# Keys and values of eight sampled tokens: float32 products in four column groups and a summing product

## The chip, the core and the metric

The kernel runs on one core of a Trainium2 chip. The metric is the device time of one launch in microseconds (us). Three runs of the kernel before gave 896.83, 897.12 and 897.53 us; the median is 897.12 us.

## What is computed

One layer of a hybrid decoder for 512 new prompt tokens and 8 sampled tokens (one new token for each of 8 sequences with a cache of 1,024 tokens). The part that the change touches is the projection of keys and values, cut from the reference:

```python
h = modulate(x, lp['norm_attn'], sh1, sc1)           # (512 + 8 tokens) x 1024
proj = jnp.dot(h, lp['w_in'])                         # 1024 x 1816
sizes = [D_SSM, D_ATTN, D_KV, D_KV, D_KV, D_KV, D_KV, D_KV]
u, q, k_c, v_c, k_s, v_s, k_w, v_w, g = jnp.split(proj, offsets, axis=-1)
```

`k_c, v_c` feed the compressed branch of the attention, `k_s, v_s` the selected one, `k_w, v_w` the window; each pair is 256 columns wide. `g` are 24 gate columns. Everything is float32 in the reference. The projected keys and values are outputs too.

## The kernel before

All tensors of the layer lie with 128 features in partitions and tokens in columns. `hH` and `hL` hold the normed input as a high and a low part in a rounded float32 form (`F32R`): 8 blocks of 128 features (`KT`), 520 columns each, the last 8 of them the sampled tokens (`T:NT`). `split` makes such a pair: ScalarE rounds a copy, VectorE subtracts. A product of two such pairs is three matmuls (high by high, high by low, low by high). Plain float32 operands are also taken by TensorE; the trace then shows two records for one matmul.

`kv_proj(c)` is called for c = 0, 1, 2 (compressed, selected, window). It loads 1 MB of `w_in` into a raw buffer (`wkv`, 1024 features by 256 columns; for c = 2 also the gate columns `rg`), splits it into `wH` and `wL`, and then, for five groups of tokens t, multiplies tokens (stationary) by weights (moving): t = 0 to 3 are 128 prompt tokens each, t = 4 is the 8 sampled tokens. Each t takes 24 matmuls, three for each of 8 feature blocks. For t = 4 the result is 8 rows by 256 (or 280) columns; ScalarE copies it to `kvs`, from which it goes to the outputs and later into the attention of the sampled tokens.

Raw buffers come from a pool of three (`rawt`), used in turn by blocks of `w_ada` (`wada`, for the modulation, `ada`), blocks of the cache (`rc`), `wkv` and others. A load into a raw buffer waits until the last reader of the block before it is done. The small buffer `mrow` has one copy; `ada` puts its sums there, and the query projection its `ql`. `ada(s)` multiplies the condition vectors by a block of `w_ada` in float32: the 8 feature blocks go in turn to four groups of 32 output partitions, and the four groups are added after a transpose (`padt`) by a reduction on VectorE.

A scheduler decides the order on each engine: it takes the instructions as written, with their dependences and its own estimate of durations, and fills each engine's queue. So a change in one place shifts what stands beside it, and what follows. Every queue (PE, ACT, DVE, POOL, and SP which issues most loads) is worked off in order, and a waiting instruction holds those behind it.

The stages in the order of time: set-up, first compressed cache blocks and input norm (to about 93 us in the profiled execution); projection `pj` of the state space input, and `kv_proj(0)` (to 136 us); the state space stage in eight steps `qd`, with the cache blocks of the sampled tokens, `ada` and the compressed branch beside it (to about 250 us), in whose last part `kv_proj(1)` and `kv_proj(2)` lie; the queries (to about 296 us); the attention (to about 450 us); then the output projection and the two large products of the MLP.

Of the state space stage these pieces matter: `uscr` is a scratch in DRAM, to which the input `u` is written (from `ut` for the prompt, from `uT` for the sampled tokens); ten loads `U<-uscr` bring it back in another layout; `pvs` (line 792) is the first product of a step that needs `U`; `mscr` and `Tz` are a second way through DRAM for each step.

In the attention, 16 rounds of the prompt (scores `pst`, exponentials on ACT, transposes `ptp`, values `po`) alternate with the work of the sampled tokens (`pkT`, `pS`, `ppt`, `poS`, `pov`) and the gates of the state space output (`pg`).

Of the kernel before, what the change touches and what calls it, by code (L numbers as in the profile page):

```python
# [9 lines left out]
F32 = mybir.dt.float32  # L10
# [3 lines left out]
ALU = mybir.AluOpType  # L14
AX = mybir.AxisListType

P = 128
D = 1024
T = 512
NB = 8  # L20
NT = T + NB
HB = NT // 2
KT = D // P
# [13 lines left out]
def body(tc, i, o, dbg=None):  # L37
    nc = tc.nc
# [18 lines left out]
    def pst(tag, name):  # L57
        return bank["tile"].tile([P, 512], F32, tag=tag, name=name, bufs=bank["tags"][tag])
# [13 lines left out]
    ident = cst.tile([P, P], F32, name="ident")  # L72
# [44 lines left out]
    wp = ctx.enter_context(tc.tile_pool(name="wp", bufs=1, reuse_waits="tile"))  # L117
    k2x = ExitStack()
    keep2 = k2x.enter_context(tc.tile_pool(name="keep2", bufs=1, reuse_waits="tile"))
    mod = keep.tile([P, 48, 9], F32, name="mod")  # L120
    xs = keep.tile([P, KT, NB], F32, name="xs")
# [78 lines left out]
        nc.scalar.activation(oh, hf, AF.Identity, bias=sh)  # L200
        nc.vector.scalar_tensor_tensor(ol, hf, sh, oh, ALU.add, ALU.subtract)

    def affine_samples(pool, oh, ol, x, bs, A, sh):

        th = pool.tile([P, KT, NB], F32, tag="ths", name="ths")
        nc.vector.tensor_tensor(th, x, bs.unsqueeze(1).to_broadcast([P, KT, NB]), ALU.mult)
        nc.vector.tensor_tensor(th, th, A[:, :, 1:9], ALU.mult)
        nc.vector.tensor_tensor(th, th, sh[:, :, 1:9], ALU.add)
        split(oh[:, :, T:NT], ol[:, :, T:NT], th)
# [287 lines left out]
    for lv in range(3):  # L497
        n = 1 << lv
# [73 lines left out]
    hH = hp.tile([P, KT, NT], F32R, name="hH")  # L572
    hL = hp.tile([P, KT, NT], F32R, name="hL")

    def x_tile(k):
        px = pst("tr", "px")
        for t in range(4):
            nc.tensor.transpose(px[:, t * P : (t + 1) * P], xr[t][:, k * P : (k + 1) * P], ident)
        xk = p0.tile([P, T], F32, tag="xk", name="xk", bufs=4)
        nc.scalar.copy(xk, px)  # L580
        nc.gpsimd.dma_start(xscr[:, k], xk)
        return xk

    affine_samples(p0, hH, hL, xs, bc[1], A1, mod[:, 0:8])
    for k in range(KT):
        affine_split(p0, hH[:, k, 0:T], hL[:, k, 0:T], x_tile(k), bc[0], A1[:, k, 0:1], mod[:, k, 0:1])
    p0x.close()
# [33 lines left out]

    onames = ("cmp", "slc", "win")

    def kv_proj(c):
        c0 = 1024 + 256 * c
        r = rawt("wkv").rearrange("p (k c) -> p k c", k=KT)
# [5 lines left out]
        ws = []  # L632
# [7 lines left out]
        for t in range(5):  # L640
            tok = slice(t * P, t * P + (P if t < 4 else NB))
            mp = P if t < 4 else NB
            ps = pst("pj", "pkv")
            for k in range(KT):
                wh, wl = ws[k // 4]
                for n, (x, w) in enumerate(((hH, wh), (hH, wl), (hL, wh))):
                    nc.tensor.matmul(ps[0:mp, 0:nw], x[:, k, tok], w[:, k % 4], start=(k == 0 and n == 0),  # L647
                                     stop=(k == KT - 1 and n == 2))
            if t == 4:
                nc.scalar.copy(kvs[:, c * 256 : (c + 1) * 256], ps[0:NB, 0:256])  # L650
                if c < 2:
# [944 lines left out]
```

## Time and profile before

| | |
|---|---|
| median of 3 runs | 897.12 us |
| profiled execution | 896.29 us, of it 894.6 us from the first to the last instruction (span) |
| TensorE busy (matmuls) | 844.3 us, 94% |
| VectorE busy | 525.0 us, 59% |
| ScalarE busy | 388.2 us, 43% |
| GpSimd busy | 65.2 us, 7% |
| chain that ended last | PE 86%, DMA 6%, ACT 3%, DVE 2% |
| DMA traffic | 122.36 MB, 137 GB/s on the mean |

The share of busy time says that TensorE is the engine to look at first, and the chain (the work that ended last, followed back from the end) says how much of the span TensorE's own work set. Line numbers, as L647, are those of the kernel before. A name as `pkv<-wH,hH` reads: tile `pkv` is written from `wH` and `hH`. The duration of one matmul in the trace reaches past the start of the next one, since matmuls are pipelined; what a matmul takes from TensorE is therefore read from the distance of two starts.

### The profile page before, as it was taken

What the parts mean: (1) busy time and instruction counts of PE and PEld (TensorE: products, weight loads), DVE (VectorE), ACT (ScalarE), POOL (GpSimd) and SP (SyncE); (2) the same over time, 40 slices, a digit from 0 to 9 for tenths busy, and PEclk for the clock granted to TensorE, in tenths of its full rate; (3) what the DMA queues carried; (4) which work ended last, traced back from release to release, by engine and by line L of the source; (5) the groups of instructions that cost most, each with busy time, mean ns of one, the idle gap of its engine ahead of it and who ended that gap; (6) DMA issues with size and microseconds to landing.
All of it is one profiled execution on the core that took longest, in us unless ns stands there. A gap on an engine that the chain in (4) does not pass through costs nothing.

```text
span 894.6 us, 16415 instructions
## 1 busy us (share of the span) xinstructions
PE 844.3 (94%) x6517; PEld 747.3 (84%) x6517; DVE 525.0 (59%) x1413; ACT 388.2 (43%) x880; POOL 65.2 (7%) x147
## 2 busy tenths in 40 slices
PE   3799998999999899999889999999999999999995
PEld 2567897788998676756579999999999999999995
DVE  6676656759747975667578964443233444434534
ACT  2545326634435656546655554441111344433422
POOL 6001201000134200100000000000000000000000
PEclk9999999999999999999999999999999999999998
DMA  8956678366456620303257552333333333332202
GB/s 294 318 193 217 194 169 239 123 204 194 127 179 206 203 95 1 142 1 142 78 206 227 161 189 85 95 95 95 95 95 95 95 95 95 96 88 70 79 1 95
DMA packets 111836, 122.36 MB, mean 137 GB/s; under 512 B 24500, under 2 KB 91880, under 8 KB 109584
## 3 DMA queue, kind: packets, MB, share of 16 engines
q1 hardware_dynamic: 102256, 89.71, 33.0%
q0 software_dynamic: 5488, 29.99, 9.8%
q10 hardware_dynamic: 4016, 1.62, 0.7%
q8 instruction: 51, 0.84, 0.4%
q14 instruction: 25, 0.20, 0.1%
HBM read 112.47 MB, written 13.03 MB: 140 GB/s over the span
## 4 chain that ended last, share of the span: by engine, by line
PE 86%; DMA 6%; ACT 3%; DVE 2%; issue 1%; SPq 0%; ACTq 0%; DVEq 0%
PE pdn L1401 21%; PE pup L1401 20%; PE pj L605 5%; PE pwo L1401 5%; PE pkv L647 5%; PE ph L387 5%; DMA wada<-w_ada 5%; PE pada L334 2%; PE ptp L1246 2%; PE po L1253 2%; PE pS L1032 2%; PE pg L1273 2%; PE pst L1217 2%; PE pys L819 2%; PE pkT L1023 1%; PE pst L1218 1%
## 5 line engine op out<-in xcount | busy, mean ns | idle before, releaser
L1401 PE MATMUL pdn<-hidL,wH 128*128 128x256 f32 (+1 forms) x480 | 136.1, 284 | 0.0
L1401 PE MATMUL pdn<-hidH,wL 128*128 128x256 f32 (+1 forms) x480 | 135.9, 283 | 0.0
L1401 PE MATMUL pdn<-hidH,wH 128*128 128x256 f32 (+1 forms) x480 | 135.4, 282 | 0.0
L1401 PE MATMUL pup<-h2L,wH 128*128 128x256 f32 (+1 forms) x480 | 135.0, 282 | 0.0
L1401 PE MATMUL pup<-h2H,wL 128*128 128x256 f32 (+1 forms) x480 | 135.0, 282 | 0.0
L1401 PE MATMUL pup<-h2H,wH 128*128 128x256 f32 (+1 forms) x480 | 134.1, 283 | 0.0
L1401 PEld LDWEIGHTS pup<-h2L,wH 128*128 128x128 f32 x480 | 90.4, 188 | 0.8 <-DVE rs_t L97 0.8
L1401 PEld LDWEIGHTS pdn<-hidH,wL 128*128 128x128 f32 x480 | 90.6, 189 | 0.0
L1401 PEld LDWEIGHTS pdn<-hidL,wH 128*128 128x128 f32 x480 | 90.4, 188 | 0.1
L1401 PEld LDWEIGHTS pup<-h2H,wL 128*128 128x128 f32 x480 | 90.4, 188 | 0.0
L1401 PEld LDWEIGHTS pdn<-hidH,wH 128*128 128x128 f32 x480 | 90.4, 188 | 0.0
L1401 PEld LDWEIGHTS pup<-h2H,wH 128*128 128x128 f32 x480 | 89.6, 188 | 0.0
L63 ACT CAST wH<-wdn 128x1024 fp32r<-128x1024 f32 x30 | 31.5, 1050 | 114.0 <-PE pdn L1401 104.1
L64 DVE TENSOR_TENSOR wL<-wup,wH 128x1024 fp32r<-128x1024 f32 x30 | 36.7, 1224 | 58.1 <-ACT wH L63 58.1
L64 DVE TENSOR_TENSOR wL<-wdn,wH 128x1024 fp32r<-128x1024 f32 x30 | 36.8, 1225 | 54.2 <-ACT wH L63 54.2
L387 PE MATMUL ph<-xc,w 128*128 128x256 f32 (+2 forms) x320 | 65.4, 356 | 1.2 <-DVE xc L377 0.7
L387 PEld LDWEIGHTS ph<-xc,w 128*128 128x128 f32 x320 | 52.8, 203 | 12.9 <-issue 6.4
L63 ACT CAST wH<-wup 128x1024 fp32r<-128x1024 f32 x30 | 31.5, 1050 | 48.0 <-PE pup L1401 37.6
L1479 ACT ACTIVATE rl<-pup 128x256 f32<-128x256 f32 (+1 forms) x64 | 24.4, 384 | 48.9 <-PE pup L1401 48.8
L375 ACT COPY xc<-pxc 64x256 f32<-64x256 f32 x96 | 32.1, 366 | 20.8 <-DVE xc L377 18.2
L1410 DVE SCALAR_TENSOR_TENSOR xT<-pdn,mod,xT 128x256 f32<-128x256 f32 x32 | 15.2, 479 | 43.2 <-PE pdn L1401 43.2
L1480 DVE TENSOR_TENSOR rl<-rl 128x256 f32<-128x256 f32 (+1 forms) x64 | 27.1, 425 | 22.6 <-ACT rl L1479 22.6
(557 smaller groups left out, 2023.9 us busy)
## 6 DMA issues: line engine op xcount, KB each, us to landing
wada<-w_ada SPq DMA_DIRECT2D x20, 1024.0 KB
wup<-w_up SPq DMA_DIRECT2D x16, 1024.0 KB
wdn<-w_down SPq DMA_DIRECT2D x16, 1024.0 KB
wo<-w_out SPq DMA_DIRECT2D x8, 1024.0 KB
wada<-w_ada SPq DMA_DIRECT2D x8, 512.0 KB
rwin<-state_win SPq DMA_DIRECT2D x4, 1024.0 KB
new_win_sample<-state_win POOLq DMA_DIRECT2D x2, 2044.0 KB, 8.9
wkv<-w_in SPq DMA_DIRECT2D x3, 1024.0 KB
```

Of the source, the lines that this page charges most:

```text
L63: nc.scalar.copy(h, src)
L64: nc.vector.tensor_tensor(l, src, h, ALU.subtract)
L334: nc.tensor.matmul(ps[k % 4 * 32 : k % 4 * 32 + 32], cT[:, k], rs[k // kp][:, k % kp], start=(k < 4), stop=(k >= 4))
L375: nc.scalar.copy(dst[:, :, :, hf], srcv[:, :, :, hf])
L387: nc.tensor.matmul(phv[:, lo:hi, 0:w], w1[n][:, r_], xc[n][:, lo:hi, r_ % 8, off : off + w], start=(r_ == 0), stop=(r_ == 15))
L605: nc.tensor.matmul(ps[:, 0:HB], w[:, k], x[:, k, hc], start=(k == 0 and n == 0), stop=(k == KT - 1 and n == 2))
L647: nc.tensor.matmul(ps[0:mp, 0:nw], x[:, k, tok], w[:, k % 4], start=(k == 0 and n == 0), stop=(k == KT - 1 and n == 2))
L819: nc.tensor.matmul(py[:, c], Tz[:, :, :, g].rearrange("p t c -> p (t c)"), U[:, qd * GQ + g], start=True, stop=False)
L1032: nc.tensor.matmul(S[b4 * 32 : b4 * 32 + 32], q4[:, 4 * grp + b4], kts[b4], start=True, stop=True)
L1401: nc.tensor.matmul(ps[:, 0 : b - a], w, x[:, a:b], start=first and n == 0, stop=last and n == 2)
L1479: nc.scalar.activation(rl, ps[:, 0 : b - a], AF.Relu)
L1480: nc.vector.tensor_tensor(rl, rl, rl, ALU.mult)
```

## The change

For t = 4 the 24 matmuls are replaced. A new tile `hs` holds the 8 sampled tokens in plain float32, padded with zeros to 32 columns for each of the 8 feature blocks. Eight float32 matmuls multiply `hs` (128 features by 32 tokens, stationary) by the raw block `wkv` itself (moving, 256 columns); feature block k goes to the group of 32 output partitions k mod 4, so each group adds two blocks. For c = 2 eight more of 24 columns do the gates from `rg`. ScalarE copies the 128 rows into `part`, which uses the buffer of `mrow`; then one float32 matmul with `sel` (128 by 8: which rows belong to token p) adds the four groups into a new PSUM tile `pks`. The rest of t = 4 is as before. `hs` is filled where the split of the sampled tokens is made; `sel` is a sum over `ident`.

```diff
-        th = pool.tile([P, KT, NB], F32, tag="ths", name="ths")
+        if th is None:
+            th = pool.tile([P, KT, NB], F32, tag="ths", name="ths")
...
+    hs = hp.tile([P, KT, 32], F32, name="hs")
+    nc.gpsimd.memset(hs, 0.0)
...
-    affine_samples(p0, hH, hL, xs, bc[1], A1, mod[:, 0:8])
+    affine_samples(p0, hH, hL, xs, bc[1], A1, mod[:, 0:8], hs[:, :, 0:NB])
...
+    sel = p1.tile([P, NB], F32, name="sel")
+    nc.vector.tensor_reduce(sel, ident.rearrange("p (q x) -> p x q", x=32)[:, 0:NB], AX.X, ALU.add)
...
-            for k in range(KT):
-                wh, wl = ws[k // 4]
-                for n, (x, w) in enumerate(((hH, wh), (hH, wl), (hL, wh))):
-                    nc.tensor.matmul(ps[0:mp, 0:nw], x[:, k, tok], w[:, k % 4], start=(k == 0 and n == 0),
-                                     stop=(k == KT - 1 and n == 2))
+            if t == 4:
+
+                for c0, src in ((0, r),) + (((256, rg),) if c == 2 else ()):
+                    for k in range(KT):
+                        q = slice(k % 4 * 32, k % 4 * 32 + 32)
+                        nc.tensor.matmul(ps[q, c0 : c0 + src.shape[2]], hs[:, k], src[:, k], start=(k < 4), stop=(k >= 4))
+                part = wp.tile([P, 520], F32, tag="mrow", name="part")[:, 0:nw]
+                nc.scalar.copy(part, ps[:, 0:nw])
+                ps = pst("pj", "pks")
+                nc.tensor.matmul(ps[0:NB, 0:nw], sel, part, start=True, stop=True)
+            else:
+                for k in range(KT):
+                    wh, wl = ws[k // 4]
+                    for n, (x, w) in enumerate(((hH, wh), (hH, wl), (hL, wh))):
+                        nc.tensor.matmul(ps[0:mp, 0:nw], x[:, k, tok], w[:, k % 4], start=(k == 0 and n == 0),
+                                         stop=(k == KT - 1 and n == 2))
```

The scheduler's order differs from the first of these places on until the MLP. Three places matter for the prediction.

The first is SP's queue where `u` goes out to `uscr` and comes back as `U`, at the end of `kv_proj(0)`. Before:

```order
L619 DMA uscr<-uT 128x8
L330 DMA wada<-w_ada 128x4x512
L618 DMA uscr<-ut 128x512
L724 DMA U<-uscr 16x32x8
L725 DMA U<-uscr 16x32x8
L722 DMA U<-uscr 16x32x64 x8
L772 DMA mscr<-M_1541 128x64
```

Now:

```order
L623 DMA uscr<-uT 128x8
L742 DMA U<-uscr 16x32x8
L622 DMA uscr<-ut 128x512
L743 DMA U<-uscr 16x32x8
L740 DMA U<-uscr 16x32x64 x8
L331 DMA wada<-w_ada 128x4x512
L790 DMA mscr<-M_1532 128x64
```

The 1 MB block `wada` (first half of `ada(5)`) goes into the raw buffer that held `wkv` of c = 0; it stood ahead of the last write to `uscr`, and now stands behind the ten loads of `U`.

The second place is TensorE's queue where the summing product of c = 1 and of c = 2 stands, and ScalarE's at c = 2. TensorE at c = 1 now:

```order
L656 MATMUL pkv<-wkv,hs 32x256 x5
L700 MATMUL pkt<-ident,kvt 128x128 x2
L785 MATMUL pbb<-ident,BP 128x128 x4
L660 MATMUL pks<-part,sel 8x256
L665 MATMUL pkv<-wH,hH 128x280
```

TensorE at c = 2 now (`pj` is the first product of the queries):

```order
L656 MATMUL pkv<-wkv,hs 32x256 x8
L656 MATMUL pkv<-rg,hs 32x24 x8
L700 MATMUL pkt<-ident,kvt 128x128 x2
L660 MATMUL pks<-part,sel 8x280
L609 MATMUL pj<-hH,wH 128x260
```

ScalarE at c = 2 before (from the copies of t = 3 to those of t = 4):

```order
L675 COPY kvt<-pkv 128x256
L677 COPY Vx<-pkv 128x128
L103 ACTIVATE gates<-pkv 128x24
L678 DMA new_win_prompt<-kvt 128x2x64
L679 DMA new_win_prompt<-Vx 128x128
L63 CAST wH<-wq 128x1024
L650 COPY kvs<-pkv 8x256
```

and now:

```order
L693 COPY kvt<-pkv 128x256
L695 COPY Vx<-pkv 128x128
L103 ACTIVATE gates<-pkv 128x24
L63 CAST wH<-wq 128x1024
L696 DMA new_win_prompt<-kvt 128x2x64
L697 DMA new_win_prompt<-Vx 128x128
L63 CAST KH<-pkt 128x2x128
L658 COPY part<-pkv 128x280
L668 COPY kvs<-pks 8x256
```

At c = 0 fourteen other matmuls stand between the products and their sum, at c = 1 six, at c = 2 two; and at c = 2 a cast of weights, two issues of stores and a cast of `KH` stand ahead of the copy `part` on ScalarE.

The third place is the end of the attention on TensorE. Before, from the last work of the sampled tokens (`pov`) to the output projection (`pwo`):

```order
L1127 MATMUL pov<-ident,ovS 128x128
L1253 MATMUL po<-PT,Vx 64x512 x2
L1246 MATMUL ptp<-ident,pe 128x128 x2
L1246 MATMUL ptp<-ident,pe_4992 128x128 x2
L1246 MATMUL ptp<-ident,pe 128x128
L1253 MATMUL po<-PT,Vx 64x384 x2
L1253 MATMUL po<-PT,Vx 64x128 x2
L1253 MATMUL po<-PT,Vx 64x256 x2
L1329 MATMUL po<-etc,Vbd 128x512
L1401 MATMUL pwo<-mixH,wH 128x256
```

Now a part of what stands between `pov` and `pwo`, 15 to 26 rows ahead of `pwo`:

```order
L1271 MATMUL po<-PT,Vx 64x384 x2
L1271 MATMUL po<-PT,Vx 64x128 x2
L1264 MATMUL ptp<-ident,pe 128x128
L1264 MATMUL ptp<-ident,pe_4854 128x128
L1264 MATMUL ptp<-ident,pe 128x128 x2
L1235 MATMUL pst<-KH,QS 128x256
L1236 MATMUL pst<-KL,QS 128x256
L1237 MATMUL pst<-cmaskr,identr 128x128
L1271 MATMUL po<-PT,Vx 64x256 x2
L1264 MATMUL ptp<-ident,pe 128x128 x3
```

Before, 12 rows lie from `pov` to `pwo`, the values of the last pair of heads; now 43 rows do, with the last scores of the prompt among them. The work of the sampled tokens has moved to earlier rounds.

## Rows read from the trace of the kernel before

**Rows 1.** The page's head: busy time, share of the span, instructions.
```profile
PE 844.3 (94%) x6517; PEld 747.3 (84%) x6517; DVE 525.0 (59%) x1413; ACT 388.2 (43%) x880; POOL 65.2 (7%) x147
```
**Rows 2.** Busy time by stage: each engine's us and instructions, then granted clock, DMA.
```profile
93.00:136.00 43.00, 43.00 (x364) 40.41 (x362) 25.01 (x68) 13.07 (x27) 4.25 (x8) 1.00 0.70 172
136.00:180.00 44.00, 40.29 (x262) 33.69 (x259) 30.24 (x79) 28.61 (x82) 4.87 (x14) 1.00 0.60 189
180.00:296.00 116.00, 114.60 (x851) 101.91 (x848) 82.40 (x207) 50.12 (x130) 27.10 (x65) 1.00 0.57 175
296.00:450.00 154.00, 143.96 (x1041) 94.48 (x1037) 103.36 (x323) 93.52 (x256) 9.42 (x19) 1.00 0.28 101
```
**Rows 3.** Timeline of TensorE, t = 4 of c = 0: start, us, what.
```profile
130.40 0.28 PE L647 MATMUL pkv<-wL,hH 128*8 128x256 f32 x1
...
132.72 0.28 PE L647 MATMUL pkv<-wH,hH 128*8 128x256 f32 x1
```
**Rows 4.** Timeline of TensorE, t = 4 of c = 2 and what follows.
```profile
263.33 0.29 PE L647 MATMUL pkv<-wH,hH 128*8 128x280 f32 x1
...
266.40 0.38 PE L682 MATMUL pkt<-ident,kvt 128*128 128x128 f32 x2
266.54 0.36 PE L605 MATMUL pj<-hH,wH 128*128 128x260 f32 x1
```
**Rows 5.** Timeline of TensorE: a float32 product in four column groups, and what follows.
```profile
134.96 1.07 PE L334 MATMUL pada<-wada,cT 128*32 128x512 f32 x8
135.96 0.44 PE L368 MATMUL pxc<-ident,rc 128*128 128x128 f32 x2
```
**Rows 6.** Timeline of TensorE: float32 products over all columns; 32-column products.
```profile
194.20 3.70 PE L387 MATMUL ph<-xc,w 128*128 128x256 f32 x16
197.74 0.34 PE L820 MATMUL pys<-Sx,Cb 128*128 128x80 f32 x2
...
438.44 1.08 PE L1121 MATMUL poS<-rslc,ptS 128*32 128x128 f32 x32
```
**Rows 7.** Timeline of ScalarE around t = 4 of c = 2.
```profile
263.67 0.38 ACT L675 COPY kvt<-pkv 128x256 f32<-128x256 f32 x1
264.08 0.39 ACTq L678 DMA_DIRECT2D new_win_prompt<-kvt  x1
264.09 0.22 ACT L103 ACTIVATE gates<-pkv 128x24 f32<-128x24 f32 x1
264.51 0.77 ACTq L679 DMA_DIRECT2D new_win_prompt<-Vx  x1
265.32 1.05 ACT L63 CAST wH<-wq 128x1024 fp32r<-128x1024 f32 x1 [1.01 <-PE pkv L647]
```
**Rows 8.** Timeline of SP, where `uscr` is written and `U` read.
```profile
120.61 0.38 SPq L330 DMA_DIRECT2D wada<-w_ada  x1
121.15 0.39 SPq L618 DMA_DIRECT2D uscr<-ut  x1
127.00 5.11 SPq L722 DMA_DIRECT2D U<-uscr  x8
```
**Rows 9.** Timeline of TensorE's weight loads, 137 to 142 us.
```profile
138.48 0.97 PEld L792 LDWEIGHTS pvs<-U,Bb 128*128 128x128 f32 x8 [1.67 <-issue]
141.53 0.16 PEld L334 LDWEIGHTS pada<-wada,cT 128*32 128x32 f32 x8 [1.31 <-DMA wada<-w_ada]
```
**Rows 10.** Timeline of TensorE at the end of the attention.
```profile
436.39 1.09 PE L1049 MATMUL ppt<-ident,tS 128*128 128x128 f32 x8 [1.06 <-ACT tS L1010]
441.05 0.42 PE L1123 MATMUL poS<-kvs,pnw 8*32 8x128 f32 x8
448.59 0.65 PE L1253 MATMUL po<-PT,Vx 128*64 128x256 f32 x4 [1.94 <-ACT PT L1249]
```
**Rows 11.** Busy time by stretch, end of the attention, columns as in rows 2.
```profile
443.00:450.00 7.00, 4.42 (x27) 2.08 (x23) 4.90 (x10) 5.66 (x14) 0.72 (x1) 0.98 1.06 368
450.00:453.00 3.00, 3.00 (x13) 2.48 (x13) 3.00 (x12) 2.00 (x6) 0.00 (x0) 0.50 1.04 386
```

More of the change, by code (lines that the diff above doesn't have):

```diff
@@ L201, in affine_split, with affine_samples @@
         nc.vector.scalar_tensor_tensor(ol, hf, sh, oh, ALU.add, ALU.subtract)
-    def affine_samples(pool, oh, ol, x, bs, A, sh):
-        th = pool.tile([P, KT, NB], F32, tag="ths", name="ths")
+    def affine_samples(pool, oh, ol, x, bs, A, sh, th=None):
+        if th is None:
+            th = pool.tile([P, KT, NB], F32, tag="ths", name="ths")
         nc.vector.tensor_tensor(th, x, bs.unsqueeze(1).to_broadcast([P, KT, NB]), ALU.mult)
```

## The prediction

> **What bounds the kernel now.** I read the page's head first, then busy time by stage, then the timelines of single places. The head shows TensorE busy for 844.3 of 894.6 us [rows 1]. By stage the reader should see where that is true without a gap: from 93 to 136 us TensorE is busy all the time, from 180 to 296 us for 114.60 of 116 us; from 136 to 180 us it idles for 3.7 us, in the attention (296 to 450 us) for 10.0 us [rows 2]. So a matmul taken away in `kv_proj` shortens the run by its own time, as long as the other engines keep up, and two of the three places of t = 4 lie in stretches where nothing but TensorE counts. The attention is another case: TensorE waits there, on and off, for ScalarE and VectorE, which are busy for 93.52 and 103.36 us of its 154 [rows 2], and what counts is which work stands beside which.
>
> **What goes.** 24 matmuls at each place. At c = 0 the rows 130.40 and 132.72 are 20 matmuls apart: 2.32 us / 20 = 0.116 us each, 24 of them 2.78 us [rows 3]; c = 1 has the same shape. At c = 2, with 280 columns, 24 starts lie from 263.33 to 266.40: 3.07 us [rows 4].
>
> **What comes on TensorE.** The eight products of `hs` by `wkv` are of a form that the trace has: `ada` multiplies 32 stationary columns by float32 weights in four column groups. One group of four with 512 columns (eight records) takes from 134.96 to 135.96, 1.00 us [rows 5]; eight with 256 columns move the same number of columns. I take 1.00 us. The upper bound is eight products one after the other at the full-width rate: 16 float32 records of 256 columns take from 194.20 to 197.74, 0.22 us a record, 0.44 us a matmul [rows 6], so 3.5 us; the lower is 0.5 us, the 16 records at 0.034 us, as in the 32 of `poS` in 1.08 us [rows 6]. The row of `ada` differs from the new products in the column count alone, so it decides. The summing product is one full-width float32 matmul, 0.44 us (0.48 us with 280 columns). The eight gate products of 24 columns are 16 records; at 0.034 us that is 0.5 us.
>
> So c = 0 and c = 1 go from 2.78 to 1.44 us, 1.34 us less each. c = 2 goes from 3.07 to 1.00 + 0.50 + 0.48 = 1.98 us, 1.09 us less.
>
> **The wait that is added.** `pks` waits for `part`, ScalarE's copy of the products (0.38 us, as the copy `kvt` of the same shape [rows 7]), and TensorE's queue stands behind it. At c = 0 fourteen other matmuls are between, and at c = 1 two transposes and four `pbb`, 6 x 0.11 us = 0.7 us: enough for the copy. At c = 2 only two transposes (0.14 us [rows 4]) are between, and ScalarE has more to do first. Counted from 263.33 us: the products end at 263.33 + 1.50 = 264.83, the transposes at 264.97. ScalarE ends `gates` at 264.31; the cast of 1,024 weight columns takes 1.05 us (to 265.36), the issue of the store of `Vx` behind it 0.77 us, of `kvt` 0.4 us (they began at 264.08 and held the queue to 265.28 [rows 7]; now they follow the start of the cast, to about 265.5), then `KH` and `part` with some 0.3 us each: 266.1 us. TensorE waits 1.1 us, does the sum to 266.6, and `pj` starts at 266.6 instead of 266.54 [rows 4]. So c = 2 saves nothing: I take 0, between a loss of 0.5 us (the cast waits for its buffer as well) and the full 1.09 us.
>
> If the copy decided at c = 0 and c = 1 too, products, copy and sum would stand in a row, 1.00 + 0.40 + 0.44 = 1.84 us, and each of the two would give 0.94 us instead of 1.34: 0.8 us less in the sum.
>
> The Trainium skill speaks for that case ("TensorEngine Tiling (Array Packing)", PSUM Bottleneck): packing products into column groups speeds TensorE up but not the copy out of PSUM, which may then be the limit. By that rule the sum below would be -1.7 instead of -2.5 us; the rows of ScalarE and the order bear it out at one place of three.
>
> **What moves.** `wkv` is now read until t = 4, so the raw buffer of c = 0 comes free some 10 us later, and the block of `w_ada` that goes into it moves behind the loads of `U`. Before, that 1 MB was issued at 120.61 us, just ahead of the last write to `uscr` at 121.15 us, and the loads of `U` could start at 127.00 us only, 5.85 us after it [rows 8]; TensorE then waited 1.67 us at `pvs`, the first reader of `U`, and 1.31 us for the next block of `w_ada` [rows 9]. Without 1 MB ahead the write should land some 3 us sooner and `U` with it. The block itself comes later, at about 131.3 us (end of the products) instead of 120.61; the one that TensorE waited for at 141.53 was issued 5.4 us before, so this one is there at 136.7 us, about when its product now comes up. Bounds: 2.98 us gained, if both waits go and none comes; 1.5 us lost, if TensorE meets the late block as early as it met the old one (134.96 us [rows 5]). I take 0.8 us gained, since TensorE gets there 1.3 us earlier and uses part of the head start up.
>
> `mrow` now holds `part` too, so the transposes of `ada(4)` move behind the sum of c = 0, and a reduction on VectorE follows before the next `ada` product: one exchange of about 0.4 us, inside the term above. The zeros of `hs` (GpSimd, 7% busy [rows 1]), `sel` and the wider copy are hidden beside TensorE.
>
> **The attention's new order.** Nothing is added there; the same work is dealt out in another way. Before, the last round still had 5 us of the sampled tokens' matmuls beside it (from `ppt` at 436.39 to `poS` at 441.05), and TensorE even so waited 1.06 and 1.94 us [rows 10], and the granted clock was 0.50 for the 3 us from 450 us, the 1.2 GHz level, after a stretch in which TensorE was busy for 4.42 of 7 us [rows 11]. Now two rounds have nothing beside them; what is gone from there fills earlier rounds. Of 10.0 us of idle time [rows 2] I let a quarter be at stake, 2.5 us either way, and take 1.0 us lost, since the tail is where ScalarE and VectorE have the least in hand.
>
> **Sum**, against the profiled execution: -1.34 - 1.34 + 0 - 0.8 + 1.0 = -2.5 us, 896.29 to 893.8 us. The median of the runs is 0.83 us above the profiled execution, so 894.6 us.
>
> **The rivals.**
> *The saving is lost in waits.* The sums wait for ScalarE at c = 0 and c = 1 too (0.8 us less, worked out with the wait), the head start of `U` is spent on the late block (0 instead of 0.8), and the attention takes 1.0 us. For it: PE's queue is in order and c = 2 shows how one cast is enough; against it: six and more matmuls stand between at the other two. -2.68 + 0.8 + 1.0 = -0.9 us: 896.2 us, no change that can be told.
> *The attention pays more.* The place is from the last `pov` to `pwo`. If the two bare rounds run at the pace of ScalarE and VectorE, the 5 us of matmuls that stood in the last round are no longer hidden, and another spell at the 1.2 GHz level, as the 3 us from 450 us (1.5 us lost), can follow. It decides as soon as it costs over 3.5 us; with 5 us, -1.34 - 1.34 - 0.8 + 5 = +1.5, with the clock +3.0 us: 898.6 to 900.1 us. For it: 12 rows have become 43 behind `pov`. Against it: what moved fills idle time elsewhere.
> *The state space stage starts 3 us sooner and keeps it.* Then both waits of rows 9 go: -2.68 - 2.98 + 0 = -5.7 us: 891.5 us. For it: SP's queue; against it: from 180 us on TensorE is nearly full, so a chain that is early has nothing to give.
>
> **How the numbers follow.** The forecast 0.46, lost in waits 0.23, slower attention 0.19, early stage 0.12. A measurement here tells 0.2% from no change, 1.8 us: faster is below 895.3, slower above 898.9 us. The forecast's own spread is 893 to 896.2 us; of its 0.46, 0.08 lie above 895.3. Faster: 0.38 of it, 0.12, and 0.02 of the case of the waits, 0.52; same: 0.08 and the other 0.21, 0.29; slower: 0.19. The range that leaves out 2 in 10 reaches from 891.2 to 899.8 us; the likeliest case alone holds 893 to 896.2.
>
> **What would show it.** Eight products of `hs` in about 1.0 us and sums of 0.44 us; a gap ahead of `pks` at c = 2 of about 1 us and none at c = 0 and c = 1; `U` loads issued near 124 us and `pvs` near 136 us instead of 138.48; the stage's end some 2 us sooner; the attention as long as before within 2.5 us; from `pwo` on the same length. I am wrong if the column groups don't run beside each other (products of 2 us and more), if `pada` waits for the late block, or if the attention differs by more than 3 us.

## The result and the profile after

The changed kernel is slower. Four runs gave 905.44, 908.79, 912.67 and 917.11 us, median 910.73 us; the kernel before gave a median of 896.98 us beside them (895.37 to 897.53). The ratio is 1.0158, 95% interval 1.0123 to 1.0194. The prediction was 894.6 us, with a range of 891.2 to 899.8 us: wrong in sign, and its range missed too.

The profiled execution is the one of 917.11 us; its head answers to [rows 1], with the granted clock in 40 slices below:

```profile
PE 857.3 (94%) x6515; PEld 756.5 (83%) x6515; DVE 528.6 (58%) x1414; ACT 390.5 (43%) x883; POOL 65.0 (7%) x148
...
PEclk9999999996999989999999999999999999999998
```

TensorE is busy for 13.0 us more than before, although it has less to do, and the tenth slice of the clock (206 to 229 us) stands at 6 tenths, the fifteenth at 8. Where the time went is read from stretches that begin and end at the same matmul in both kernels: the first `pkv` of c = 0, the last `pj`, the first `pwo`, the first `pup` and the first `pdn`. The windows of the kernel before (stretch, us, then busy us and instructions of PE, PEld, DVE, ACT, POOL, then granted clock, DMA share, GB/s); the third row is the last part of the second, from the last `pov` on:

```profile
118.20:295.47 177.27, 172.16 (x1259) 151.71 (x1259) 123.91 (x324) 82.68 (x219) 31.44 (x76) 1.00 0.61 177
295.47:449.81 154.34, 144.30 (x1041) 94.36 (x1041) 103.69 (x324) 93.82 (x256) 9.95 (x23) 1.00 0.28 100
442.29:449.81 7.52, 4.55 (x27) 2.09 (x27) 5.33 (x13) 6.18 (x14) 0.96 (x1) 0.99 1.04 352
449.81:503.47 53.66, 52.08 (x414) 50.78 (x413) 44.80 (x129) 28.63 (x52) 0.00 (x0) 0.97 0.61 197
503.47:602.85 99.38, 98.95 (x823) 95.18 (x822) 57.22 (x133) 45.13 (x98) 0.00 (x0) 1.00 0.40 122
```

The same stretches of the changed kernel, and four short ones that are spoken of further down:

```profile
116.08:303.93 187.85, 182.69 (x1261) 156.70 (x1261) 120.77 (x315) 82.08 (x220) 26.29 (x68) 0.94 0.56 163
303.93:465.33 161.40, 146.56 (x1042) 97.61 (x1041) 110.12 (x338) 96.28 (x260) 14.62 (x31) 0.96 0.34 116
446.09:465.33 19.24, 14.04 (x80) 7.97 (x79) 12.67 (x38) 13.78 (x35) 0.00 (x0) 0.91 0.66 232
465.33:521.33 56.00, 52.06 (x414) 51.06 (x412) 45.44 (x129) 29.83 (x55) 0.00 (x0) 0.97 0.47 151
521.33:623.66 102.33, 100.92 (x821) 96.87 (x821) 56.02 (x130) 44.85 (x97) 0.00 (x0) 0.98 0.37 114
...
131.85:134.28 2.43, 0.01 (x1) 0.04 (x1) 2.32 (x6) 1.67 (x5) 0.00 (x0) 1.00 1.05 374
134.28:141.10 6.82, 6.42 (x29) 4.36 (x29) 2.87 (x9) 3.88 (x12) 0.32 (x1) 0.50 0.26 67
209.40:212.80 3.40, 3.40 (x29) 3.08 (x26) 3.37 (x10) 1.40 (x3) 0.61 (x2) 1.00 0.72 226
212.80:229.80 17.00, 17.00 (x84) 15.41 (x86) 9.31 (x26) 3.67 (x7) 0.47 (x3) 0.50 0.34 107
```

The span grew by 915.4 - 894.6 = 20.8 us: -2.1 up to the first `pkv` (where the kernel before had 3.4 us at a granted clock of 0.50 and the changed one none), +10.6 to the last `pj`, +7.1 in the attention, +2.3 in the output projection, +2.9 (2.95) to the first `pdn`, and nothing behind it. Three things are to be seen.

First, the places that the change edits are not where the time went. TensorE's timeline of the changed kernel (start, us, engine, line, operation, tile, form, count; in brackets the idle time before it and what ended it):

```profile
128.26 1.07 PE L656 MATMUL pkv<-wkv,hs 128*32 128x256 f32 x16
129.26 0.40 PE L784 MATMUL pm<-C,BP 128*128 128x16 f32 x2
...
131.25 0.60 PE L660 MATMUL pks<-part,sel 128*8 128x256 f32 x2
...
134.27 1.95 PE L810 MATMUL pvs<-U,Bb 128*128 128x72 f32 x8 [2.42 <-DVE BP L772]
...
274.94 1.07 PE L656 MATMUL pkv<-wkv,hs 128*32 128x256 f32 x16
...
277.38 0.64 PE L660 MATMUL pks<-part,sel 128*8 128x280 f32 x2 [0.88 <-ACT part L658]
277.95 0.39 PE L609 MATMUL pj<-hH,wH 128*128 128x260 f32 x1
...
450.55 0.50 PE L1235 MATMUL pst<-KH,QS 128*128 128x512 f32 x1 [1.99 <-ACT pe L1245]
...
457.86 1.23 PE L1264 MATMUL ptp<-ident,pe 128*128 128x128 f32 x8 [1.44 <-DVE pe L1250]
459.82 1.08 PE L1271 MATMUL po<-PT,Vx 128*64 128x512 f32 x4 [0.73 <-ACT PT L1267]
...
518.62 0.61 PE L1390 MATMUL bc<-dg,ones 128*128 128x128 f32 x4
521.33 0.50 PE L1419 MATMUL pup<-h2H,wH 128*128 128x256 f32 x2 [2.11 <-ACT h2H L200]
522.79 0.39 PE L1419 MATMUL pup<-h2L,wH 128*128 128x256 f32 x1 [0.72 <-DVE h2L L201]
```

The products take 129.26 - 128.26 = 1.00 us, the sum waits for nothing at c = 0 and c = 1 and 0.88 us at c = 2. The loads of `U` [rows 8] begin earlier, and the block of `w_ada` follows them, as SP's queue now shows:

```profile
121.84 6.21 SPq L740 DMA_DIRECT2D U<-uscr  x8
129.39 0.40 SPq L331 DMA_DIRECT2D wada<-w_ada  x1
```

From the first `pkv` to `pvs` it takes 134.27 - 116.08 = 18.19 us; before, `pvs` stood 20.3 us behind the first `pkv` (its weights at 138.48 [rows 9], `pkv` at 118.20). TensorE's share of it, before and now:

```profile
118.20:138.48 20.28, 18.85 (x162) 16.99 (x161) 13.15 (x43) 6.83 (x18) 0.00 (x0) 1.00 0.87 159
...
116.08:134.27 18.19, 15.77 (x141) 14.37 (x139) 12.98 (x43) 5.79 (x14) 0.00 (x0) 1.00 0.87 154
```

It is busy for 3.08 us less and idles for 0.99 us more. Less than half of the 3.08 us is the products: eight records each of `pada` (at 134.96 before [rows 5], at 139.18 now) and of `pxc`, some 2 us, stood ahead of `pvs` and now stand behind it.

Second, the end of the attention: from the last `pov` to the first `pwo` 19.24 us instead of 7.52. There are 62 matmul instructions in it instead of 18 (transposes and the last `pov` counted; the list of the old order shown ahead of the prediction has 15 of the 18), TensorE idles 5.2 us instead of 3.0, and the granted clock is 0.91. Over the whole attention TensorE idles 14.84 us instead of 10.04 and is busy 2.26 us longer: 4.80 + 2.26 = 7.06 us.

Third, between `pwo` and `pdn`. The broadcast `bc` of the second norm's scale ended 25 `pwo` matmuls ahead of `pup` before; now all `pwo` stand ahead of its last four, and `pup` waits 2.11 us for `h2H`, then 0.72 us for `h2L`. The two rows of TensorE's timeline before, for `bc` and `pup`:

```profile
500.20 0.38 PE L1372 MATMUL bc<-dg,ones 128*128 128x128 f32 x2
...
503.47 0.40 PE L1401 MATMUL pup<-h2H,wH 128*128 128x256 f32 x2
```

Up to the first `pdn` the changed kernel spends 44.4 us at a granted clock of 0.50, the 1.2 GHz level, where the kernel before spends 6.8 us.

### The profile page after: what moved, and what is told of

Its sections match the earlier page's. It is cut to its first block, busy times and chain, and to the rows that moved or that the text cites. A ratio compares the mean times of both kernels' runs of the same rounds, so it can differ in the third digit from the quotient of the medians.

```text
span 915.4 us, 16406 instructions
## 1 busy us (share of the span) xinstructions
PE 857.3 (94%) x6515; PEld 756.5 (83%) x6515; DVE 528.6 (58%) x1414; ACT 390.5 (43%) x883; POOL 65.0 (7%) x148
## 4 chain that ended last, share of the span: by engine, by line
PE 64%; DVE 2%; ACT 2%; DMA 1%; issue 1%; ACTq 0%; DVEq 0%
PE pup L1419 20%; PE pdn L1419 20%; PE pwo L1419 5%; PE pj L609 3%; PE ptp L1264 2%; PE po L1271 2%; PE pg L1291 2%; PE pst L1235 1%; PE pS L1050 1%; PE pkT L1041 1%; PE pst L1236 1%; PE poS L1139 1%; DMA rslc<-cache_slc,pidx 1%; PE psc L1177 1%; PE pfin L1523 0%
## 5 line engine op out<-in xcount | busy, mean ns | idle before, releaser
L388 PEld LDWEIGHTS ph<-xc,w 128*128 128x128 f32 x320 | 52.2, 200 | 10.5 <-issue 4.9
L1245 ACT ACTIVATE pe<-pst,mxa 128x512 f32<-128x512 f32 (+1 forms) x64 | 33.7, 533 | 16.0 <-DVE mxa L1241 15.7
```

Of the source, the lines that this page charges most:

```text
L388: nc.tensor.matmul(phv[:, lo:hi, 0:w], w1[n][:, r_], xc[n][:, lo:hi, r_ % 8, off : off + w], start=(r_ == 0), stop=(r_ == 15))
L1245: nc.scalar.activation(at(qt, 0, nk), d, AF.Exp, bias=mx[:, qt : qt + 1], accum_out=dn[:, qt : qt + 1])
```

## The experiments

The theory after the first profile: the new products are as cheap as predicted, and the loss is the scheduler's new order (its waits, and the clock that falls in them). The rivals: the products and their waits themselves; the raw block that is held longer; the one pause of 2.43 us at 132 us and what the clock does after it. To hold an order, a helper takes the instructions as traced on an engine, puts them in the order of a table, and ties each to the next without a wait; it stands at the end of the kernel for PE, ACT, DVE, POOL and SP (the tables, lists of numbers, are left out):

```diff
+def hold_order(tc, table, engine):
+    nc = tc.nc
+    traced = [x for x in nc.cur_bb.bb.instructions
+              if x.engine == engine and x.opcode not in ("RegisterMove", "TilePoolBoundary")]
...
+    for a, b in zip(order, order[1:]):
+        tc.add_manual_dep(b, a.name, no_wait, reason="hold_order")
...
+        hold_order(tc, ORDER_PE, mybir.EngineType.PE)
```

Times are medians beside runs of the kernel before on the same chip (897.65, 896.53 and 896.73 us in the three series, 57 runs from 894.31 to 905.32 us, nine of them above 900). Holding an order costs nothing that shows by itself: two kernels below that are held ("filled pause" and "freed") run as the changed kernel and as the one before. The last table of this section has the stages of each.

**Old products, new order.** The kernel before, with each engine held to the changed kernel's order: `hs`, `part` and `pks` are missing, and the 24 matmuls stand where the products stand now.

> Before's 24 split products per block, but every engine's instructions stand in the order of the changed kernel. Theory A (order: the time went into the order in which the engines' work now stands, through longer waits and more time at 1.2 GHz): slow as the changed kernel or a little more, 905 to 920 us, granted clock 0.97 to 0.985. Theory B (the new products: column groups of fp32 products and a sum that waits for ScalarE are what is slow or lowers the clock): as the kernel before, 895 to 899 us, clock 0.99.

916.24 us, ratio 1.0188 (1.0127 to 1.0250): the whole loss is there without one of the new instructions, and with the raw blocks released at their split, as before. It is some 6 us above the changed kernel, as it would be if the new products saved time in this order; but the ranges of the runs overlap, and four runs of each do not show it.

**New products, old order.** The products, with their copy to a buffer of its own, stand at the start of the block's work, the sum at t = 4; every engine is held to the order of before.

```diff
+        pss = pst("pj", "pkv")
+        for c0, src in ((0, r),) + (((256, rg),) if c == 2 else ()):
+            for k in range(KT):
+                q = slice(k % 4 * 32, k % 4 * 32 + 32)
+                nc.tensor.matmul(pss[q, c0 : c0 + src.shape[2]], hs[:, k], src[:, k], start=(k < 4), stop=(k >= 4))
+        part = p1.tile([P, 280], F32, tag="part", name="part")[:, 0:nw]
+        nc.scalar.copy(part, pss[:, 0:nw])
...
-                part = wp.tile([P, 520], F32, tag="mrow", name="part")[:, 0:nw]
```

> The new products, but every engine's instructions stand in the order of the kernel before; the products of a block stand ahead of its prompt products, so that the raw weights are released as early as before, their sum stands where the 24 products stood, and the copy of the partial sums has a buffer of its own. Theory A (order): the saving of the products alone shows, 892 to 895.5 us, granted clock 0.99, three blocks shorter by 1.3 us each. Theory B (the new products are what is slow): 903 us or more.

902.64 us, 1.0045 (1.0019 to 1.0071), outside the range of either theory. More than half of the loss is gone; attention, `pwo` and `pup` are as long as before (154.2, 53.9, 99.4 us). But the gain isn't there, and the stretch to `pj` is 3.1 us longer. The timelines tell why. TensorE's:

```profile
227.05 0.69 PE L836 MATMUL pys<-U,Tz 128*128 128x80 f32 x2 [1.06 <-DMA Tz<-mscr]
...
270.36 0.39 PE L609 MATMUL pj<-hH,wH 128*128 128x260 f32 x1 [1.64 <-ACT wH L63]
```

SP's of the same kernel:

```profile
220.64 0.37 SPq L634 DMA_DIRECT2D wkv<-w_in  x1
221.10 1.55 SPq L791 DMA_DIRECT2D Tz<-mscr  x1
```

TensorE's just before, `wada` and the products of c = 1:

```profile
219.51 1.92 PE L335 MATMUL pada<-wada,cT 128*32 128x512 f32 x16
221.25 1.05 PE L651 MATMUL pkv<-wkv,hs 128*32 128x256 f32 x16
```

and ScalarE's:

```profile
269.27 1.04 ACT L63 CAST wH<-wq 128x1024 fp32r<-128x1024 f32 x1 [0.56 <-ACT kvs L667]
```

Before, SP issued these two loads at 216.41 and 216.94 us, the first of them right after VectorE had split the second `wkv` block (to 216.38 us). The products still need that block at 221.25 us. The load of the third block now stands ahead of them, at 220.64 us, and follows the first eight records of `pada` (to 220.57 us), so it can't have the buffer of the second block as before, and takes that of a `wada` block. `Tz` stands behind it, 4.2 us late; `pys` pauses 1.06 us, and soon after it the clock is at 0.50 for 3.4 us (228.60 to 232.00 us). At c = 2 the 24 old matmuls were the time in which ScalarE cast the first weights of the queries; without them `pj` waits 1.64 us.

**New products, old order, freed.** The same, with both waits mended in the held order: on SP `Tz` and the store to `yscr` stand ahead of the third `wkv` load; on ScalarE and VectorE the first split of the query weights stands ahead of the last copies of c = 2.

> The new products in the old order as in the first run of that kind, with two places mended that its trace showed: in the SyncE queue the second block's Tz load stands ahead of the third block's weight load, which waits for a buffer (Tz came 4.2 us late, TensorE paused 1.06 us and fell to 1.2 GHz for 3.4 us); and at the third block ScalarE and VectorE split the query weights before they evict the last prompt tile (TensorE paused 1.64 us there). If these two waits took what the products saved: 3 to 5 us shorter than that run, 895 to 898 us, no such pauses. If the saving is lost elsewhere: as that run, 901 to 904 us.

895.93 us, 0.9982 (0.9959 to 1.0005), and again, in a later series:

> The mended kernel with the new products in the old order, once more without an edit, for a narrower interval: 894 to 898 us, 0.1 to 0.4% faster than the kernel before, among its runs some with a granted clock of 0.986 to 0.989 that are 3 us longer.

896.69 us, 0.9994 (0.9967 to 1.0022). Neither `pys` nor `pj` waits now:

```profile
229.01 0.58 PE L836 MATMUL pys<-U,Tz 128*128 128x80 f32 x2
...
268.81 0.39 PE L609 MATMUL pj<-hH,wH 128*128 128x260 f32 x1
```

So with the order of before and both waits mended the products cost nothing, and some 14 us come back. But they aren't seen to gain either: the 24 runs of this kernel have a median of 896.31 us and reach from 892.66 to 901.14. In the first profiled execution the clock fell in another place, with no wait ahead of it (the third row is the same stretch in the second profile):

```profile
206.70:210.10 3.40, 3.40 (x34) 3.40 (x32) 3.40 (x12) 0.82 (x2) 0.50 (x2) 1.00 0.90 298
210.10:223.70 13.60, 13.60 (x68) 12.06 (x71) 9.07 (x24) 4.70 (x10) 0.48 (x3) 0.50 0.14 36
...
210.10:223.70 13.60, 13.60 (x116) 12.98 (x119) 11.48 (x32) 5.70 (x13) 0.98 (x5) 1.00 0.56 184
```

**Products first, free order.** The same edit as in "new products, old order" (products early, `part` in a buffer of its own, so no exchange with `ada`'s `mrow`), but the scheduler is left free.

> The same products, early in their block and with a buffer of their own for the partial sums, but the order is left to the scheduler again. Theory A (order): any time between 893 and 915 us, to be told by the waits and the clock of whatever order comes out. Rival C (what hurts is that the raw weights are held until the new tokens' products, which delays the loads behind them): 897 us or less, since they are released early here.

910.03 us, 1.0117 (1.0071 to 1.0162): neither the copy's buffer nor the products' place was the cause. The scheduler deals out a third order, with 17.1 us from the last `pov` to `pwo`.

**Filled pause.** The changed kernel in its own order, with ten 512-column matmuls into an unused tile behind the products of c = 0, which fill the pause before `pvs`.

```diff
+    fill = pst("pj", "fill")
+    for n in range(10):
+        nc.tensor.matmul(fill, hH[:, 0, 0:P], hH[:, n % KT, 0:T], start=True, stop=True)
```

> The changed kernel in its own order, with ten 128x512 products whose result nobody reads behind the first block's sum, where TensorE paused from 131.85 to 134.27 us ahead of a spell of 6.8 us at 1.2 GHz. If the pause is what lowered the clock: the spell at 134 us is gone and the run is some 3 us shorter than the changed kernel (905 to 908 us, the other spells left). If the clock falls for another reason: the spell stays, and the time is that of the changed kernel or up to 1 us more.

911.38 us, 1.0145 (1.0095 to 1.0195). The stretch that stood at 0.50 is at full clock, but the run is not shorter. Another spell follows later, at a place where the changed kernel's first profile has none; the fourth row shows that the changed kernel's second profile (below) has it without the fill:

```profile
134.90:141.00 6.10, 5.31 (x43) 3.95 (x42) 4.01 (x12) 4.87 (x15) 1.58 (x2) 1.00 0.40 93
172.40:175.80 3.40, 2.60 (x21) 2.60 (x22) 3.20 (x11) 3.29 (x11) 0.70 (x2) 1.00 1.06 325
175.80:182.60 6.80, 5.15 (x25) 2.95 (x23) 3.43 (x10) 5.48 (x16) 0.18 (x2) 0.50 0.52 170
...
175.98:182.81 6.83, 5.86 (x29) 3.78 (x27) 3.88 (x12) 6.08 (x18) 0.58 (x3) 0.50 0.57 180
```

One pause, then, isn't the cause of the loss. That it sets off the spell behind it fits: both profiles of the changed kernel have one there (6.8 and 3.4 us), this one has none.

**The changed kernel again.** Unchanged, with a new profile.

> The changed kernel once more, without an edit, for the other kernels of this group and for the clock. Theory A: waits that come from the order stand at the same instructions as in the first profile (the stretch from the last pov to the first pwo 19 us long, a pause of 2 us ahead of the first pup), and 905 to 917 us; the stretches at 1.2 GHz are partly others, above all the 17 us at 213 us, which need not come again, since the run with the filled pause had none there. If the order had no fixed waits, these stretches would scatter by several us.

909.77 us, 1.0148 (1.0092 to 1.0205). The attention, `pwo` and `pup` stretches are the same to 0.5 us (160.9, 56.0, 102.3); the stretch to `pj` is 181.4 instead of 187.9 us, with 10.2 instead of 23.9 us at 0.50. The stretch that was slow from 212.8 us on ran at full clock this time:

```profile
206.00:233.00 27.00, 27.00 (x210) 22.76 (x210) 20.77 (x61) 10.10 (x24) 1.85 (x7) 1.00 0.69 217
```

**Halves of the order.** Two kernels are held to the order of one up to the queries and of the other behind them, each on all five engines. The first has the new products and the old late order; the second is the kernel before with the changed kernel's late order.

> The changed kernel, its work up to the queries in its own order, and all work that is traced behind them (attention, output projection, feed-forward) in the order of the kernel before. Theory A (the loss sits in the order of attention, 7.1 us, and in the start of the feed-forward part, 5.3 us): 12 us shorter than the changed kernel, 894 to 901 us, last pov to first pwo 7.5 us again, no pause ahead of pup. Rival D (the loss sits ahead of that, in the blocks of keys and values and the state space, whose order is kept here): 905 us or more.

> The kernel before, with nothing changed in its products and its order up to the queries, but with all work behind them in the order of the changed kernel. Theory A: attention 7 us and the start of the feed-forward part 5 us longer, 907 to 913 us, though no part of the change is in it. Rival D: within 2 us of the kernel before.

The second gave 911.56 us, 1.0124 (1.0076 to 1.0172): with all of the old products, the late order is as slow as the change, and the stages from `pj` on are those of the changed kernel (159.9, 56.0, 102.3 us). They are 10.8 us longer than before, of 15.7 us in this profile; 4.4 us of the rest stand ahead of them, where the joint of the two orders makes a wait of 3.17 us (1.4 before), with 6.8 us at 0.50 around it:

```profile
283.45 0.58 PE L605 MATMUL pj<-hH,wH 128*128 128x260 f32 x1 [3.17 <-ACT QS L913]
```

The first gave 908.99 us, 1.0145 (1.0092 to 1.0198), which missed what I expected of it and lies where rival D has it. But its end is as before (7.5 us from `pov` to `pwo`, 53.1, 99.4), and here too the joint made a wait of its own, at the start of the attention:

```profile
310.39 0.62 PE L1014 MATMUL pgs<-gates,e8q 8*128 8x24 f32 x2 [6.16 <-DVE gsel L1017]
```

With it, and 10.2 us at 0.50, the attention takes 164.3 us, 10.0 more than before, of the 10.5 us by which this profile's span is longer. So the time of this kernel doesn't tell what the new early order is worth, though its stretch up to `pj`, ahead of the joint, does; it also shows how dear an order is that doesn't fit what came before it.

**One block only.** The change at c = 1 alone, and at c = 2 alone; the other two places keep their 24 matmuls, and the scheduler is free. The first kernel's edit (the second has `c == 2`):

```diff
-            if t == 4:
+            if t == 4 and c == 1:
```

> The change in the second block (c=1) alone, scheduled freely; the other two blocks keep their 24 products. The order that comes out has 38 matrix products between the last pov and the first pwo (18 in the kernel before, 62 in the changed one) and none of the last four bc ahead of the end of pwo. Theory A (the scheduler's order of the late part costs, whatever set it off): 903 to 912 us although the products of one block can save 1.3 us at most. If the loss needs all three blocks' new products: within 2 us of the kernel before.

> The change in the third block (c=2) alone, scheduled freely. Its order is that of the kernel before up to the end of the second block, and that of the changed kernel in attention and behind it. Theory A: 905 to 913 us, last pov to first pwo 19 us, a pause of 2 us ahead of pup. If the loss needs the first two blocks: within 2 us of the kernel before.

907.26 us, 1.0107 (1.0063 to 1.0152), and 909.68 us, 1.0132 (1.0074 to 1.0189). A third of the change brings most of the loss, at either place: it doesn't grow with the number of products. The last part of the attention of the second one answers to the 7.52 and 19.24 us above:

```profile
434.55:456.37 21.82, 15.37 (x79) 9.18 (x79) 12.72 (x38) 13.77 (x35) 0.00 (x0) 0.84 0.59 206
```

In the orders as built there are, counted as above, 18 matmul instructions from the last `pov` to the first `pwo` before, 62 in the changed kernel, 41 with the products first, 38 with c = 1 alone and 62 with c = 2 alone.

**Freed, with fill.** The freed kernel, with ten 512-column matmuls dealt out between the narrow `php` products where the clock had fallen (210 to 224 us).

```diff
+        fill = pst("po", "fill")
...
+                if r_ % 2 and (n or r_ > 11):
+                    nc.tensor.matmul(fill, hH[:, r_ // 2, 0:P], hH[:, r_ // 2, 0:T], start=True, stop=True)
```

> The mended kernel with ten 128x512 products, whose result nobody reads, between the 128x62 products php, where its first profile had 13.7 us at 1.2 GHz without a pause of TensorE. They cost 10 x 0.22 = 2.2 us. If a row of such narrow products lowers the clock: no run has that stretch, all runs at a granted clock of 0.991 or more and within 3 us of each other, median 896 to 898 us. If it comes from something else: the same share of runs at 0.986 to 0.989, median 898 us or more.

898.36 us, 1.0016 (0.9997 to 1.0035). The stretch keeps its clock in this profile, as it did without the fill in the freed kernel's second one:

```profile
210.10:223.70 13.60, 13.60 (x111) 11.69 (x114) 11.32 (x33) 5.11 (x12) 0.50 (x4) 1.00 0.28 84
```

The runs lie closer (896.99 to 900.40 us), but not lower: spells elsewhere remain (mean clock 0.988 to 0.995, where 0.991 or more was expected), and the fill is work as well. So this doesn't show that the fill keeps the clock up. No version tried beats the kernel before by more than can be measured.

The stages in the profiled executions, us between the same matmuls as above (from the ends of `pj` and `pov`, from the starts of the others); in brackets the us at a granted clock of 0.50:

| kernel | to `pkv` | to last `pj` | to `pwo` | of it behind `pov` | to `pup` | to `pdn` | span |
|---|---|---|---|---|---|---|---|
| before | 118.2 | 177.3 (0) | 154.3 (0) | 7.5 | 53.7 | 99.4 | 894.6 |
| changed | 116.1 | 187.9 (23.9) | 161.4 (13.7) | 19.2 | 56.0 | 102.3 | 915.4 |
| changed, again | 116.8 | 181.4 (10.2) | 160.9 (13.7) | 19.3 | 56.0 | 102.3 | 909.2 |
| old products, new order | 118.4 | 182.3 (3.4) | 161.6 (13.7) | 19.5 | 55.9 | 102.3 | 912.2 |
| old products, late part new | 118.6 | 181.7 (6.8) | 159.9 (10.2) | 19.3 | 56.0 | 102.3 | 910.3 |
| new products, late part old | 117.8 | 178.7 (3.4) | 164.3 (10.2) | 7.5 | 53.1 | 99.4 | 905.1 |
| products first, free order | 117.1 | 183.5 (17.1) | 162.4 (17.1) | 17.1 | 54.3 | 102.3 | 911.4 |
| filled pause | 116.8 | 181.3 (6.8) | 161.6 (13.7) | 19.5 | 55.9 | 102.3 | 909.6 |
| c = 1 only | 117.9 | 180.3 (17.1) | 160.7 (13.7) | 12.8 | 56.0 | 100.8 | 907.5 |
| c = 2 only | 118.6 | 175.1 (3.4) | 162.7 (13.7) | 21.8 | 56.0 | 102.3 | 906.4 |
| new products, old order | 119.0 | 180.4 (3.4) | 154.2 (0) | 7.5 | 53.9 | 99.4 | 898.6 |
| freed | 116.5 | 182.1 (13.7) | 154.9 (1.1) | 8.1 | 53.2 | 99.4 | 897.9 |
| freed, again | 118.3 | 180.4 (10.2) | 154.3 (0) | 7.5 | 53.2 | 99.4 | 897.3 |
| freed, with fill | 118.0 | 179.2 (3.4) | 154.8 (1.2) | 8.0 | 53.2 | 99.4 | 896.3 |

The columns behind `pov`, to `pup` and to `pdn` are short (7.5 to 8.1, 53.1 to 53.9, 99.4 us) wherever the late part stands in the order of before, and longer in every other order, whichever products a kernel has.

## Why the prediction was wrong

**The terms of the products and their sums were right.** Products: 1.00 us predicted, 1.00 measured. The sum, from its start to that of the next matmul at c = 2: 0.48 predicted, 277.95 - 277.38 = 0.57 measured. The wait at c = 2: about 1.1 us predicted, 0.88 measured; at c = 0 none, as predicted. So the rule of the Trainium skill weighed there ("TensorEngine Tiling (Array Packing)", PSUM Bottleneck) held at the one place that I had allowed it. The loads of `U` were predicted near 124 us and issued from 121.84 on. From `pkv` to `pvs` I had -1.34 - 0.8 = -2.1 us, and the profiles show 18.19 - 20.3 = -2.1, but that is luck. The 0.8 stood for shorter waits, and TensorE waits 2.42 us at `pvs` instead of 1.46 (1.67 is the pause of its weight loads [rows 9]). The stretch is shorter because some 2 us of other work moved behind `pvs`. `pvs` itself came at 134.27 instead of "near 136".

**The step that failed is "The attention's new order".** I had put a quarter of the idle time at stake and taken +1.0 us; it is +7.1 in the first profile and +6.6 in the repeat. The rival that pays more named the right place, from `pov` to `pwo`, but its price, 5 us of matmuls no longer hidden and 1.5 us for one spell of the clock, was for that place alone. There it was 11.7 us, and the earlier rounds, which got the sampled tokens' matmuls, gave back only 4.7 of it (142.2 us from `pj` to `pov` instead of 146.8). That the net 7.1 lies near this rival's 6.5 is thus not its price confirmed. I had read the order and counted 12 rows against 43, and let "what moved fills idle time elsewhere" pay for it. That the old products with the late order alone have nearly the same stages (159.9, 56.0, 102.3 against 161.4, 56.0, 102.3) shows that this is the order's price and not the products'.

**"From `pwo` on the same length" failed too**, by 2.3 + 2.9 = 5.3 us. I had followed the order to `pwo` and no further. The same reading, carried on to the next place where TensorE needs another engine's result, would have shown the last `bc` with no `pwo` matmul behind it to cover the norm.

**The clock was taken as one spell of 3 us; it was 44.4 us at the 1.2 GHz level.** In the runs of the changed kernel a mean clock of 0.972, 0.978, 0.983 and 0.986 goes with 917.11, 912.67, 908.79 and 905.44 us: 11.67 us for 0.014, some 8 us for each hundredth. Straight lines of one slope through the runs of before, changed and changed again, freed, and old products in the new order have 7.3 us for a hundredth, and at an equal clock of 0.99 leave the changed kernel 5.3 us above the one before, the old products in the new order 9.0 us above, and the freed kernel 0.6 us below. So of the some 13 us lost in the medians, 7 to 8 are the clock, by that fit, and 5 to 6 are what the waits cost beyond what the products save. It is a fit and not an experiment: no kernel here has the new order at full clock. The waits by themselves are read from the rows above: in the first profile TensorE's idle time from the first `pkv` to the first `pdn` grew by 8.2 us, from 17.16 to 25.35 us.

**The stretch up to the queries** is where I had put the gain. In three profiles with the new products and the new early order it takes 187.9, 181.4 and 178.7 us, with 23.9, 10.2 and 3.4 us at 0.50, where before had 177.3 us and none: what it lost goes with the clock, about half a us for each us at 0.50. If that half is taken off everywhere, it takes 175.9 to 177.0 us in those three, 180.6 us with the old products in the new order, 177.3 us before and 175.3 us in both profiles of the freed kernel: the products give some 4 us in the new order and 2 in the old one, and the new early order takes 3.3. My sum had -2.68 for c = 0 and c = 1 and 0 for c = 2, so its size is borne out roughly and no closer. This is an estimate from single profiles.

**What the predicted time was right for.** 894.6 us is close to what the freed kernel does (895.93 and 896.69 us); but neither is told apart from before, so the gain of 2.5 us is not confirmed either. To get there the order had to be held by hand and two covers replaced which the 24 matmuls and their early release of the raw block had provided. I had asked what the matmuls cost and not what they hid.

**What stays open.** Which estimate of the scheduler tips it into the late order isn't settled: one block's products suffice (c = 1 or c = 2). What the new early order costs by itself is known as the estimate above only, since the kernel for it got a wait of 6.16 us at its joint. And why the clock falls where it does is not settled (below).

## What to carry to other kernels

Where a scheduler deals out the order, a small edit can move work a hundred microseconds away: count what stands between the last work that hides a chain and the next result TensorE must wait for, in the old and the new order, at every such place down to the end, and take that for a term as large as the edit itself. Before taking work from the bounding engine, ask which cast, load or copy ran beside it. And to learn what an edit itself is worth, hold the order fixed and change the edit, then hold the edit fixed and change the order.

## What the hardware did that I had not expected

The granted clock fell to 0.50 in two kinds of places. One is a pause: TensorE had idled from 131.85 to 134.28 us, and the clock was at 0.50 from 134.28 on. Behind the queries too, each fall of the changed kernel follows a wait; the one at 523.40 us follows the 2.11 and 0.72 us of `pup`. The Trainium skill ("TensorE: Matmul & The Clock Gate", section "HAM oscillation — how this bites in real kernels") puts such falls down to gaps in which TensorE idles. The row at 134.28 us agrees in kind, with a gap of 2.42 us, shorter than those that the section describes. The other kind is not a pause: from 209.40 to 212.80 us TensorE was busy for 3.40 of 3.40 us, and from there it was at 0.50 for 17 us, with matmuls all the time; that section has no such case. What ran there in the changed kernel are `php` products of 62 columns:

```profile
209.72 1.77 PE L715 MATMUL php<-xTp,w 128*128 128x62 f32 x14
...
222.60 5.22 PE L715 MATMUL php<-xTp,w 128*128 128x62 f32 x24
```

One record takes 1.77 / 14 = 0.13 us ahead of the fall and 5.22 / 24 = 0.22 us in it. The same stretch fell, with TensorE busy throughout, in two more of the fourteen profiles: in the freed kernel's first (13.6 us, above) and with c = 1 alone:

```profile
213.78:227.44 13.66, 13.66 (x66) 10.74 (x64) 9.47 (x23) 4.58 (x10) 0.58 (x3) 0.50 0.15 34
```

In the other eleven it stood at full clock, the repeats of the changed and the freed program among them, and the `php` products ran there in all of them. So these products alone don't set it off, and what does stays open.

Nor had I expected that spells of one program come and go between its executions, above all in the stretch up to the queries (23.9 and 10.2 us in two profiles), so that the changed kernel's first four runs spread over 12 us. The kernel before does this too, only more seldom: its four runs beside them lie within 2.2 us, but its 57 runs of the later series within 11. The spells in the attention (13.7 us) stood in both profiles of the changed kernel; the profile of before has next to none there.
